# A two-layer fp32 decoder trunk on one core: the first loads put into one queue, and the last columns finished block by block

## The chip, the core and the metric

The kernel runs on one core of a Trainium2 chip. The core has a matrix engine (TensorE, PE in the profile, with its weight loads as PEld), a vector engine (VectorE, DVE), a scalar engine (ScalarE, ACT), GpSimd (POOL) and SyncE (SP), which here only issues DMAs. All five run their own instruction streams and wait for one another through semaphores. The metric is device time in microseconds for one execution, the median of several. TensorE has two clock levels, 1.2 and 2.4 GHz; the profile gives the granted clock as a share of the upper one.

## What is computed

256 tokens (T) of width 2048 (D) pass two layers and a final normalisation, all in float32:

```python
for i in range(DEPTH):                       # 2 layers
    x = x + mixer(rmsnorm(x, mix_g))         # layer 0: stick-breaking attention || gated short convolution
                                             # layer 1: chunked spatial gate || forgetting attention
    x = x + conv_ffn(rmsnorm(x, ffn_g), w_up, conv_w, w_down)
return rmsnorm(x, final_norm_g)

def rmsnorm(x, g):
    return x * lax.rsqrt(jnp.mean(x * x, axis=-1, keepdims=True) + EPS) * g
def conv_ffn(h, w_up, conv_w, w_down):       # w_up 2048 x 11264, w_down 5632 x 2048
    gate, up = jnp.split(causal_dwconv(h @ w_up, conv_w), 2, axis=-1)
    return (jax.nn.silu(gate) * up) @ w_down
```

The weights, some 400 MB in all, are each read once.

## The kernel before, in words

**Tiles.** The residual stream `res[b][g]` stays on the core: two blocks of 128 tokens (b), each in four column groups of 512 (g). Weights come as `raw` tiles of 512 rows by 512 columns (1 MB, `load`, L216) over SP's DMA queue; five `raw` buffers turn round. ACT casts each half of a tile to a rounded `hi` (L233), DVE subtracts to get the rest, `lo` (L234). The activations are held in the same way as a pair hi|lo, `xg` (16 tiles of 128 features, `make_xg`, L186) or `act`.

**Products.** `gemm` (L248) makes features by tokens: for each k-tile (128 rows of the weight) and each of four output tiles one matmul of `hi` with 512 columns (the activation's hi and lo side by side, L238) and one of `lo` with 256 (L241). `gemm_tok` (L277) makes tokens by columns: per k-tile and block three matmuls with 512 columns (L291 to L293). A normalisation's factor is applied after the product, so the first projection needs only x transposed and multiplied by the gain; the row sums of squares are needed later.

**Order.** The code calls each step in a program order; a scheduler then sorts each engine's instructions by that order and its own estimates of when inputs are there. Side jobs (`active`, `waiting`) advance by one step after each half weight tile (`tick`).

**The head.** x comes in eight DMAs of 256 KB (L417), the first weight tile in four of 256 KB, the next two in halves, interleaved on SP's queue by the list `START`. ACT's queue brings the first gain `g0row` (L130), six small rows of other gains into `vrow` (L431 to L433), and, hoisted to the start by the scheduler, `fb` (L531) and `sgb` (L542, 512 KB). `bring_x` transposes one column group of x on PE (L196, tiles `px`), makes four `xg` tiles of it (ACT L188, DVE L189) and squares it on ACT (`squares`, L184, tiles `junk`), two k-tiles of the first projection at a time.

**The tail.** `ffn` (L482) runs 11 up-projection steps in chunks; `down(ci)` multiplies a chunk's result by its rows of `w_down` and adds to `res`. The last call covers three steps, [8, 9, 10], so 12 k-tiles for each column group g. After g's two sums (L339, one a block) `final(g)` squares both blocks (L184) and multiplies them by the final gain (L718). When g = 3 is done for both blocks, eight small operations give the two factors per token (L722, L164 to L172), and block 0's four groups are scaled on DVE (L730), block 1's on ACT (L732), each sent by its own DMA of 256 KB (L733, SP for block 0, ACT for block 1).

Of the kernel before, what the change touches and what calls it, by code (L numbers as in the profile page):

```python
# [36 lines left out]
START = [("x", 0), ("w", 0), ("x", 1), ("w", 1), ("x", 2), ("w", 2), ("x", 3), ("w", 3)]  # L37
# [3 lines left out]
def trunk(  # L41
# [55 lines left out]

    ident = cp.tile([P, P], F32, name="ident")
# [30 lines left out]
    g0row = cp.tile([KD, P], F32, name="g0row")  # L129
    nc.scalar.dma_start(g0row, l0_mix_norm_g.rearrange("(r p) -> r p", p=P))  # L130
# [44 lines left out]
    res = [[cp.tile([P, 512], F32, tag=f"res{b}{g}", name=f"res{b}{g}") for g in range(4)] for b in range(2)]  # L175
# [5 lines left out]
    def squares(g):  # L181
        for b in range(2):
            junk = actp.tile([P, 512], F32, tag="act", name=nm("junk"))
            nc.scalar.activation(junk, res[b][g], AF.Square, accum_out=sst[:, b, g:g + 1])  # L184
# [6 lines left out]

    def to_features(g, i):
        for n in range(4):
            px = at("px")
            for b in range(2):
                nc.tensor.transpose(px[:, b * P:(b + 1) * P], res[b][g][:, n * P:(n + 1) * P], ident)  # L196
            make_xg(px[:, :T], g * 4 + n, i)
# [17 lines left out]

    def load(w, r0, col0, halves=False):  # L216
        raw = rawp.tile([P, 4, 512], F32, tag="raw", name=nm("raw"))
        src = w[r0:r0 + 512, col0:col0 + 512].rearrange("(k p) n -> p k n", p=P)
        if halves:
            step = 1 if halves == 2 else 2  # L220
            for k in range(0, 4, step):
                nc.sync.dma_start(raw[:, k:k + step], src[:, k:k + step])
        else:
            nc.sync.dma_start(raw, src)
        return raw
# [51 lines left out]
    def gemm_tok(w, row0, col0, acts, order=None):  # L277
# [17 lines left out]
        return pss  # L295

# [113 lines left out]
    xr = x.rearrange("(b p) d -> p b d", p=P)  # L410

    for what, j in START:
        if what == "w":
            early.append(load(l0_w_in, j * 512, 0, 2 if j == 0 else j < 3))
            continue
        for b in range(2):
            nc.sync.dma_start(res[b][j], xr[:, b, j * 512:(j + 1) * 512])  # L417

    def bring_x(j):
        if j == 0:  # L420
            pv = at("pv")
            nc.tensor.transpose(pv[:, :KD], g0row, ident[:KD, :KD])
            nc.vector.tensor_copy(g0, pv[:, :KD])
# [58 lines left out]
    def ffn(w_up, conv_w, w_down, done, before=lambda: None):  # L482
# [279 lines left out]
```

## Time and profile before

| what | value |
|---|---|
| time of three runs | 2201.64, 2202.65, 2202.7 us (median 2202.65) |
| the profiled execution: its own time | 2203.05 us |
| its span (first to last instruction) | 2201.3 us |
| PE busy | 2182.9 us, 99% of the span, 11568 matmuls |
| DVE busy, ACT busy | 1471.3 us (67%), 1168.6 us (53%) |
| data moved by DMA | 411.24 MB, 187 GB/s on average |

The span is cut into three stretches for what follows: a head of 30 us, a tail that begins when the last matmul hands over at 2188.7 us, and the middle between them. "Busy" counts an engine's instructions from start to end; matmuls overlap in the array, so that a row of one matmul of 512 columns shows 0.40 us although a new one can start every 0.24 us. A row of a timeline that says x4 stands for four instructions in a row, its length for all four. The bracket at the end of a row is the idle time before it and what ended that.

### The profile page before, as it was taken

The numbers are of one execution on the slowest core, as the hardware profiler recorded it, in microseconds if no ns is written. First come the engines' busy times: TensorE is split into PE (matmuls) and PEld (weight loads), VectorE is DVE, ScalarE is ACT, GpSimd is POOL, SyncE is SP. The second block draws the span as 40 slices with busy tenths as digits, with TensorE's granted clock in tenths as the row PEclk, the third lists the DMA queues.
The fourth block names the chain that finished last, engine by engine and source line by source line (L and its number), as shares of the span: only waits on it lengthen the run. The fifth ranks groups of instructions, "written<-read, shape, count | busy, mean of one in ns | idle before, by whom it ended". The sixth has DMA issues, their size and how long they took to land.

```text
span 2201.3 us, 29434 instructions
## 1 busy us (share of the span) xinstructions
PE 2182.9 (99%) x11568; PEld 1869.9 (85%) x11568; DVE 1471.3 (67%) x2233; ACT 1168.6 (53%) x1719; POOL 5.0 (0%) x18
## 2 busy tenths in 40 slices
PE   8999999999999999999999999999999999999997
PEld 7888888888888888888888888888888888888886
DVE  5556665777667576775655568567785766757675
ACT  6566454655455454554555456555554545545453
POOL 0000000000000000000000000000000000000000
PEclk9999999999999999999999999999999999999999
DMA  8555555555555555555555555655555555555552
GB/s 297 173 173 172 188 186 184 190 191 186 192 190 182 198 185 194 186 174 192 190 190 185 171 172 184 201 176 188 191 192 191 191 191 187 195 189 189 195 173 96
DMA packets 209633, 411.24 MB, mean 187 GB/s; under 512 B 8790, under 2 KB 10454, under 8 KB 209494
## 3 DMA queue, kind: packets, MB, share of 16 engines
q1 hardware_dynamic: 204560, 405.82, 54.6%
q10 hardware_dynamic: 4934, 3.54, 0.5%
q8 instruction: 90, 1.47, 0.3%
q14 instruction: 49, 0.40, 0.1%
HBM read 407.24 MB, written 2.10 MB: 186 GB/s over the span
## 4 chain that ended last, share of the span: by engine, by line
PE 98%; DMA 1%; ACT 0%; DVE 0%; issue 0%; SPq 0%; ACTq 0%
PE mm L238 40%; PE mm L241 20%; PE mm L291 12%; PE mm L293 12%; PE mm L292 12%; PE px L196 1%; DMA raw<-in_l_w_in_dram 0%; PE po L352 0%; DMA vrow<-in_l_sc_conv_w_dram 0%; DMA res<-in_x_dram 0%; PE s L608 0%; PE pf L573 0%; PE pm L688 0%; PE po L353 0%; PE zA L369 0%; ACT res L732 0%
## 5 line engine op out<-in xcount | busy, mean ns | idle before, releaser
L234 DVE TENSOR_TENSOR lo<-raw,hi 128x1024 fp32r<-128x1024 f32 (+1 forms) x770 | 940.0, 1221 | 653.9 <-ACT hi L233 651.9
L233 ACT CAST hi<-raw 128x1024 fp32r<-128x1024 f32 (+1 forms) x770 | 807.6, 1050 | 891.5 <-PE mm L238 473.6
L238 PE MATMUL mm<-xg,hi 128*128 128x512 f32 x3840 | 1209.3, 397 | 0.0
L241 PEld LDWEIGHTS mm<-xg,lo 128*128 128x128 f32 x3840 | 717.7, 188 | 166.2
L241 PE MATMUL mm<-xg,lo 128*128 128x256 f32 x3840 | 756.4, 278 | 0.0
L238 PEld LDWEIGHTS mm<-xg,hi 128*128 128x128 f32 x3840 | 589.4, 189 | 5.2 <-ACT hi L233 0.4
L291 PE MATMUL mm<-hi,act 128*128 128x512 f32 x960 | 373.8, 390 | 0.0
L292 PE MATMUL mm<-lo,act 128*128 128x512 f32 x960 | 373.5, 389 | 0.0
L293 PE MATMUL mm<-hi,act 128*128 128x512 f32 x960 | 373.3, 390 | 0.0
L293 PEld LDWEIGHTS mm<-hi,act 128*128 128x128 f32 x960 | 180.3, 188 | 37.3
L292 PEld LDWEIGHTS mm<-lo,act 128*128 128x128 f32 x960 | 180.3, 188 | 36.8
L291 PEld LDWEIGHTS mm<-hi,act 128*128 128x128 f32 x960 | 180.3, 188 | 36.3
L314 ACT COPY y<-mm 128x256 f32<-128x256 f32 x240 | 88.7, 370 | 48.2 <-PE mm L241 48.1
L315 DVE TENSOR_TENSOR y<-mm,y 128x256 f32<-128x256 f32 x240 | 95.4, 417 | 4.5 <-ACT y L314 4.4
L317 DVE TENSOR_TENSOR y<-y,rstd 128x256 f32<-128x256 f32 x224 | 89.3, 420 | 2.0
L327 ACT ACTIVATE cv<-y,cw 128x256 f32<-128x256 f32 x176 | 80.1, 505 | 12.0 <-DVE y L317 10.6
L330 DVE SCALAR_TENSOR_TENSOR cv<-y,cw,cv 128x254 f32<-128x254 f32 x176 | 80.3, 477 | 0.0
L328 DVE SCALAR_TENSOR_TENSOR cv<-y,cw,cv 128x255 f32<-128x255 f32 x176 | 76.7, 477 | 0.0
L291 PE MATMUL mm<-hi,xg 128*128 128x512 f32 x192 | 75.3, 392 | 0.0
L292 PE MATMUL mm<-lo,xg 128*128 128x512 f32 x192 | 75.2, 391 | 0.0
L293 PE MATMUL mm<-hi,xg 128*128 128x512 f32 x192 | 74.9, 390 | 0.0
L339 DVE TENSOR_TENSOR res<-mm,res 128x512 f32<-128x512 f32 x96 | 61.6, 683 | 11.7 <-PE mm L293 11.7
(204 smaller groups left out, 723.0 us busy)
## 6 DMA issues: line engine op xcount, KB each, us to landing
raw<-in_l_ffn_up_dram SPq DMA_DIRECT2D x176, 1024.0 KB, 4.9
raw<-in_l_ffn_down_dram SPq DMA_DIRECT2D x88, 1024.0 KB, 5.1
raw<-in_l_w_in_dram SPq DMA_DIRECT2D x85, 1024.0 KB, 5.1
raw<-in_l_w_out_dram SPq DMA_DIRECT2D x32, 1024.0 KB, 5.1
res<-in_x_dram SPq DMA_DIRECT2D x8, 256.0 KB, 4.2
raw<-in_l_w_in_dram SPq DMA_DIRECT2D x4, 512.0 KB, 7.6
raw<-in_l_w_in_dram SPq DMA_DIRECT2D x4, 256.0 KB, 2.7
gfin<-in_final_norm_g_dram ACTq DMA_DIRECT2D x2, 512.0 KB, 4.7
```

The lines of the kernel that those rows point to most:

```text
L233: nc.scalar.copy(hi[:, c], rawv[:, c])
L234: nc.vector.tensor_tensor(out=lo[:, c], in0=rawv[:, c], in1=hi[:, c].bitcast(F32), op=ALU.subtract)
L238: nc.tensor.matmul(ps, lhsT=hi, rhs=a.rearrange("p s t -> p (s t)"), start=start, stop=False)
L241: nc.tensor.matmul(ps[:, :T], lhsT=lo, rhs=a[:, 0, :], start=False, stop=stop)
L291: nc.tensor.matmul(pss[b], lhsT=ah, rhs=hi[:, k, :], start=first, stop=False)
L292: nc.tensor.matmul(pss[b], lhsT=ah, rhs=lo[:, k, :], start=False, stop=False)
L293: nc.tensor.matmul(pss[b], lhsT=al, rhs=hi[:, k, :], start=False, stop=last)
L314: nc.scalar.copy(y, ps[:, T:])
L315: nc.vector.tensor_tensor(out=y, in0=ps[:, :T], in1=y, op=ALU.add)
L317: nc.vector.tensor_mul(y, y, rstd)
L327: nc.scalar.activation(a, y, AF.Copy, scale=wc(2))
L330: nc.vector.scalar_tensor_tensor(out=a[:, 2:], in0=y[:, :T - 2], scalar=wc(0), in1=a[:, 2:], op0=ALU.mult, op1=ALU.add)
```

## The change

It has five parts.

1. All of x and the first four weight tiles go through SP's queue in a fixed order, written ahead of everything else: 256 columns of x for both blocks, the first k-tile of the weight, the next 256 columns of x, the second k-tile, and so on. `res` becomes four tiles [128, 2, 512] that hold both blocks, and one DMA brings both. On ACT's queue only `g0row` is left at the start: before each of the loads of `vrow`, `fb` and `sgb` stands a small DVE copy from `rstd` into the destination, so they can't start before the first normalisation's factor exists.
2. The first weight tile is worked off k-tile by k-tile (`first_rows`): per k-tile its `xg`, its cast, its subtraction, four `hi` and four `lo` matmuls. Two k-tiles' transposes share one PSUM tile, here and in later normalisations.
3. The squares leave `bring_x`; a side job `row_sums` makes them, one column group a step, and then runs the normalisation's task.
4. Layer 1's feed-forward part has the chunks [6, 7, 8] and [9, 10] at its end in place of [6, 7] and [8, 9, 10]; the down-projection of the chunk of three is called after the first step of the last chunk, not after the second.
5. The last column group of the last down-projection is done by `gemm_by_block`: its two weight tiles are split into the 16 buffers of `xg`, free by then, first for all eight k-tiles; then come all 24 matmuls of block 0, then the 24 of block 1. `leave(b, ps)` finishes a block behind its matmuls and sends it: the sum, the squares of group 3, six small operations on one column (the sums of groups 0 to 2 are already added up in `part`), four scalings, four DMAs. Group 3's gain is multiplied in the same instruction as its scaling.

```diff
+    g0row = cp.tile([KD, P], F32, name="g0row")
+    nc.scalar.dma_start(g0row, l0_mix_norm_g.rearrange("(r p) -> r p", p=P))
+    nc.sync.dma_start(rest[0][:, :, :256], xr[:, :, :256])
+    nc.sync.dma_start(early[0][:, :1], first_w[:, :1])
+    nc.sync.dma_start(rest[0][:, :, 256:], xr[:, :, 256:512])
+    nc.sync.dma_start(early[0][:, 1:2], first_w[:, 1:2])
+    nc.sync.dma_start(early[0][:, 2:], first_w[:, 2:])
+    for j in range(1, 4):
+        nc.sync.dma_start(rest[j], xr[:, :, j * 512:(j + 1) * 512])
+        early.append(load(l0_w_in, j * 512, 0, ((0, 2), (2, 4)) if j == 1 else ((0, 4),)))
...
+    def first_rows(pss, raw, pre):
+        pieces = transposed(0)
+        for k in range(4):
+            make_xg(pieces[k], k, 0)
...
+            nc.scalar.copy(h, raw[:, k])
+            nc.vector.tensor_tensor(out=l, in0=raw[:, k], in1=h.bitcast(F32), op=ALU.subtract)
+            for n in range(4):
+                mm_hi(pss[n], h[:, n * P:(n + 1) * P], xg[k], k == 0)
+            for n in range(4):
+                mm_lo(pss[n], l[:, n * P:(n + 1) * P], xg[k], False)
+            if k == 1:
+                pre(1)
...
+    def gemm_by_block(w, row0, col0, acts, done):
+        parts = []
+        for j in range(len(acts) // 4):
+            raw = load(w, row0 + j * 512, col0)
+            for k in range(4):
+                kt = j * 4 + k
+                hi, lo = (cp.tile([P, 2, T], F32R, tag=f"xg{i}", name=nm("wl")).rearrange("p s t -> p (s t)")
+                          for i in (kt, kt + 8))
+                nc.scalar.copy(hi, raw[:, k])
+                nc.vector.tensor_tensor(out=lo, in0=raw[:, k], in1=hi.bitcast(F32), op=ALU.subtract)
+                parts.append((hi, lo))
+        for b in range(2):
+            ps = new_ps()
+            for kt, act in enumerate(acts):
...
+            done(b, ps)
...
+    def row_sums():
...
+        for g in range(4):
+            squares(g, shared=junk if g < 2 else None)
+            yield 1
+        yield from norm_task(0)
     def bring_x(j):
...
         to_features(j, 0)
-        squares(j)
-        if j == 3:
-            active.append(norm_task(1))
+        if j == 1:
+            active.append(row_sums())
     def vectors():
+        nc.vector.tensor_copy(vrow, rstd[:NV, :P])
...
-        chunks = [[0, 1], [2, 3], [4, 5], [6, 7], [8, 9, 10]]
+        chunks = [[0, 1], [2, 3], [4, 5], [6, 7, 8], [9, 10]] if tail else [[0, 1], [2, 3], [4, 5], [6, 7], [8, 9, 10]]
...
+        if g == 2:
+            nc.vector.tensor_reduce(out=part, in_=sst[:, :, :3], axis=AX.X, op=ALU.add)
+            nc.vector.tensor_scalar(out=part, in0=part, scalar1=1.0 / D, scalar2=EPS, op0=ALU.mult, op1=ALU.add)
...
+    def leave(b, ps):
+        with tc.high_priority(offset=HP):
+            nc.vector.tensor_add(res[b][3], ps, res[b][3])
+            squares(3, (b,))
...
+            for g in (0, 1, 2, 3):
+                y = res[b][g]
+                if g == 1:
+                    nc.scalar.activation(y, y, AF.Copy, scale=q)
+                elif g == 3:
+                    nc.vector.scalar_tensor_tensor(out=y, in0=y, scalar=q, in1=gfin[1][:, 512:], op0=ALU.mult,
+                                                   op1=ALU.mult)
+                else:
+                    nc.vector.tensor_scalar(out=y, in0=y, scalar1=q, scalar2=None, op0=ALU.mult)
+                (nc.scalar if g == 1 else nc.sync).dma_start(outr[:, b, g * 512:(g + 1) * 512], y)
```

**The head, SP's queue, before.** `res00` is block 0, group 0; `raw_2`, `raw_3` and `raw_4` are the first three weight tiles.

```order
L417 DMA res00_119<-in_x_dram 128x512
L417 DMA res10_123<-in_x_dram 128x512
L222 DMA raw_2_132<-in_l0_w_in_dram 128x512 x4
L417 DMA res01_120<-in_x_dram 128x512
L417 DMA res11_124<-in_x_dram 128x512
L222 DMA raw_3_139<-in_l0_w_in_dram 128x2x512 x2
L417 DMA res02_121<-in_x_dram 128x512
L417 DMA res12_125<-in_x_dram 128x512
L222 DMA raw_4_144<-in_l0_w_in_dram 128x2x512 x2
L417 DMA res03_122<-in_x_dram 128x512
L417 DMA res13_126<-in_x_dram 128x512
```

And now, the same place; `res0` is group 0 of both blocks, `raw_1` the first weight tile:

```order
L111 DMA res0_85<-in_x_dram 128x2x256
L112 DMA raw_1_91<-in_l0_w_in_dram 128x512
L113 DMA res0_85<-in_x_dram 128x2x256
L114 DMA raw_1_91<-in_l0_w_in_dram 128x512
L115 DMA raw_1_91<-in_l0_w_in_dram 128x2x512
L117 DMA res1_86<-in_x_dram 128x2x512
L101 DMA raw_2_98<-in_l0_w_in_dram 128x2x512 x2
L117 DMA res2_87<-in_x_dram 128x2x512
L101 DMA raw_3_102<-in_l0_w_in_dram 128x4x512
L117 DMA res3_88<-in_x_dram 128x2x512
L101 DMA raw_4_105<-in_l0_w_in_dram 128x4x512
```

The first weight piece has moved from third place to second, the second half of group 0 stands behind it, and groups 1 to 3 come as one DMA each.

**The head, ACT, before:** the rows around the second weight tile (`raw_3`); `xg_24` to `xg_30` are the k-tiles of x's second group, `xg_38` and `xg_40` those of the third.

```order
L188 ACTIVATE xg_24_211<-px_23_208,g0_117 128x256
L188 ACTIVATE xg_26_217<-px_25_214,g0_117 128x256
L188 ACTIVATE xg_28_223<-px_27_220,g0_117 128x256
L233 CAST hi_47_306<-raw_3_139 128x1024
L184 ACTIVATE junk_45_302,sst_127<-res02_121 128x512
L184 ACTIVATE junk_46_304,sst_127<-res12_125 128x512
L188 ACTIVATE xg_30_229<-px_29_226,g0_117 128x256
L233 CAST hi_49_326<-raw_4_144 128x1024
L233 CAST hi_61_374<-raw_4_144 128x1024
L188 ACTIVATE xg_38_281<-px_37_278,g0_117 128x256
L188 ACTIVATE xg_40_287<-px_39_284,g0_117 128x256
L184 ACTIVATE junk_59_370,sst_127<-res03_122 128x512
```

And now, first the rows of the second weight tile (`raw_2`): `xg_19`, `20`, `21` and `22` belong to x's second group, in PE's order of use 19, 20, 21, 22; `xg_32` and `xg_33` to the third.

```order
L252 CAST hi_27_237<-raw_2_98 128x1024
L252 CAST hi_36_283<-raw_2_98 128x1024
L210 ACTIVATE xg_19_197<-px_17_187,g0_137 128x256
L210 ACTIVATE xg_21_203<-px_18_192,g0_137 128x256
L210 ACTIVATE xg_32_271<-px_30_261,g0_137 128x256
L210 ACTIVATE xg_20_200<-px_17_187,g0_137 128x256
L210 ACTIVATE xg_22_206<-px_18_192,g0_137 128x256
L210 ACTIVATE xg_33_274<-px_30_261,g0_137 128x256
```

Then the rows that follow, with the third and fourth weight tiles (`raw_3`, `raw_4`) and the last two k-tiles of the third group (`xg_34`, `xg_35`):

```order
L206 ACTIVATE junk_41_327,sst_139<-res2_87 128x512
L252 CAST hi_38_305<-raw_3_102 128x1024
L252 CAST hi_48_351<-raw_3_102 128x1024
L206 ACTIVATE junk_29_257,sst_139<-res0_85 128x512
L206 ACTIVATE junk_50_371,sst_139<-res3_88 128x512
L206 ACTIVATE junk_51_373,sst_139<-res3_88 128x512
L210 ACTIVATE xg_34_277<-px_31_266,g0_137 128x256
L206 ACTIVATE junk_29_257,sst_139<-res0_85 128x512
L252 CAST hi_52_375<-raw_4_105 128x1024
L252 CAST hi_58_407<-raw_4_105 128x1024
L206 ACTIVATE junk_29_257,sst_139<-res1_86 128x512
L210 ACTIVATE xg_35_280<-px_31_266,g0_137 128x256
```

A k-tile of the third group (`xg_32`, from the transposes `px_30`) now stands ahead of the second k-tile of the second group (`xg_20`), and ahead of the third group's last one, `xg_35`, stand four casts and six squares (`junk`; a seventh, `junk_40`, is the row just ahead of this piece).

**The tail, DVE, before:** from the last column group's two sums on; `sm` are the small tiles.

```order
L339 TENSOR_TENSOR res03_122<-mm_3183_18982,res03_122 128x512
L339 TENSOR_TENSOR res13_126<-mm_3184_18983,res13_126 128x512
L718 TENSOR_TENSOR res03_122<-res03_122,gfin_3008_17926 128x512
L718 TENSOR_TENSOR res13_126<-res13_126,gfin_3008_17926 128x512
L722 TENSOR_REDUCE sm_3202_19094<-sst_127 128x2
L164 TENSOR_SCALAR sm_3204_19097<-sm_3202_19094 128x2
L168 RECIPROCAL sm_3206_19101<-sm_3205_19099 128x2
L169 TENSOR_TENSOR sm_3205_19099<-sm_3206_19101 128x2
L170 TENSOR_TENSOR sm_3205_19099<-sm_3205_19099,sm_3204_19097 128x2
L171 TENSOR_SCALAR sm_3205_19099<-sm_3205_19099 128x2
L172 TENSOR_TENSOR sm_3203_19096<-sm_3206_19101,sm_3205_19099 128x2
L730 TENSOR_SCALAR res00_119<-res00_119,sm_3203_19096 128x512
```

And now, block 1's part, which follows block 0's same nine rows:

```order
L796 TENSOR_TENSOR res3_88<-mm_3177_19061,res3_88 128x512
L799 SCALAR_TENSOR_TENSOR sm_3179_19089<-sst_139,part_12704 128x1
L802 RECIPROCAL sm_3181_19091<-sm_3180_19090 128x1
L803 SCALAR_TENSOR_TENSOR sm_3182_19092<-sm_3181_19091,sm_3179_19089 128x1
L804 TENSOR_SCALAR sm_3182_19092<-sm_3182_19092 128x1
L805 TENSOR_TENSOR sm_3182_19092<-sm_3182_19092,sm_3181_19091 128x1
L814 TENSOR_SCALAR res0_85<-res0_85,sm_3182_19092 128x512
L814 TENSOR_SCALAR res2_87<-res2_87,sm_3182_19092 128x512
L811 SCALAR_TENSOR_TENSOR res3_88<-res3_88,sm_3182_19092,gfin_2973_17887 128x512
```

The two blocks' sums no longer stand side by side, the two gain products are gone from between the squares and the factor, and the row of four scalings has become two and one that takes the gain with it.

## Rows read from the trace of the kernel before

**Rows 1.** Windows: stretch, sum; busy us of PE, PEld, DVE, ACT, POOL; PEclk; DMA share, GB/s.
```profile
0.00:30.00 30.00, 23.50 (x122) 19.19 (x123) 18.04 (x40) 21.84 (x45) 2.66 (x15) 1.00 0.90 311
30.00:2188.70 2158.70, 2158.70 (x11445) 1850.46 (x11444) 1447.81 (x2179) 1142.59 (x1665) 2.34 (x3) 1.00 0.55 185
2188.70:2201.30 12.60, 0.67 (x3) 0.20 (x2) 5.48 (x15) 4.17 (x9) 0.00 (x0) 0.66 0.45 166
```

**Rows 2.** Waits of PE: tile, line, releaser; total us, times, longest.
```profile
PE pv L422 <- DMA g0row<-in_l_mix_norm_g_dram: 3.6, 1, 3.6
PE px L196 <- DVE xg L189: 2.1, 3, 1.1
```

**Rows 3.** Timeline of PE, head: start, length, instruction, [idle before <-releaser].
```profile
5.49 0.90 PE L196 MATMUL px<-ident,res 128*128 128x128 f32 x3 [0.80 <-DMA res<-in_x_dram]
...
7.84 3.78 PE L238 MATMUL mm<-xg,hi 128*128 128x512 f32 x8
11.42 1.20 PE L241 MATMUL mm<-xg,lo 128*128 128x256 f32 x8
...
17.26 0.44 PE L196 MATMUL px<-ident,res 128*128 128x128 f32 x2 [1.14 <-DVE xg L189]
...
18.92 0.40 PE L238 MATMUL mm<-xg,hi 128*128 128x512 f32 x1
19.16 0.40 PE L241 MATMUL mm<-xg,lo 128*128 128x256 f32 x2
...
24.22 0.44 PE L196 MATMUL px<-ident,res 128*128 128x128 f32 x2 [0.25 <-DVE xg L189]
```

**Rows 4.** Timeline of ACT, head.
```profile
3.76 0.63 ACT L184 ACTIVATE junk<-res 128x512 f32<-128x512 f32 x1 [1.01 <-DMA res<-in_x_dram]
...
6.10 0.46 ACT L188 ACTIVATE xg<-px,g 128x256 fp32r<-128x256 f32 x1
...
7.17 0.62 ACT L233 CAST hi<-raw 128x512 fp32r<-128x512 f32 x1
...
24.11 0.64 ACT L184 ACTIVATE junk<-res 128x512 f32<-128x512 f32 x1
...
24.72 0.48 ACT L188 ACTIVATE xg<-px,g 128x256 fp32r<-128x256 f32 x1
...
25.52 2.00 ACT L233 CAST hi<-raw 128x1024 fp32r<-128x1024 f32 x2
```

**Rows 5.** Timeline of DVE, head.
```profile
6.58 1.27 DVE L189 SCALAR_TENSOR_TENSOR xg<-px,g,xg 128x256 fp32r<-128x256 f32 x3 [2.56 <-ACT xg L188]
7.82 1.90 DVE L234 TENSOR_TENSOR lo<-raw,hi 128x512 fp32r<-128x512 f32 x3
```

**Rows 6.** Chain that ended last, head: start us, us, what.
```profile
7.45 4.95 DMA vrow<-in_l_sc_conv_w_dram
```

**Rows 7.** DMA of 0 to 45 us, rate in 40 equal slices.
```profile
GB/s 0 55 276 257 382 255 287 193 241 325 219 401 371 251 259 340 402 410 406 390 390 395 377 384 391 382 388 388 390 384 386 386 382 386 362 206 35 0 138 391
```

**Rows 8.** Timeline of all engines, tail.
```profile
2188.72 1.37 DVE L339 TENSOR_TENSOR res<-mm,res 128x512 f32<-128x512 f32 x2 [7.84 <-PE mm L293]
...
2189.45 0.63 ACT L184 ACTIVATE junk<-res 128x512 f32<-128x512 f32 x1 [9.82 <-DVE res L339]
...
2190.21 1.37 DVE L718 TENSOR_TENSOR res<-res,gfin 128x512 f32<-128x512 f32 x2
...
2191.49 0.15 DVE L722 TENSOR_REDUCE sm<-sst 128x2 f32<-128x8 f32 x1
...
2193.11 1.68 DVE L730 TENSOR_SCALAR res<-res,sm 128x512 f32<-128x512 f32 x4
2193.63 2.48 SPq L733 DMA_DIRECT2D out_dram<-res  x4
...
2195.09 2.18 ACTq L733 DMA_DIRECT2D out_dram<-res  x2
```

**Rows 9.** DMA of 2185 to 2201.3 us, rate in 40 equal slices.
```profile
GB/s 0 0 0 0 0 0 0 0 0 0 0 0 0 0 0 0 0 0 0 0 0 0 0 266 382 367 382 387 377 362 392 377 372 392 382 387 322 0 0 0
```

More of the change, by code (lines that the diff above doesn't have):

```diff
@@ L179, in trunk, with squares @@
     xg = [None] * KD
-    def squares(g):
-        for b in range(2):
-            junk = actp.tile([P, 512], F32, tag="act", name=nm("junk"))
+    def squares(g, blocks=(0, 1), shared=None):
+        for b in blocks:
+            junk = shared
+            if shared is None:
+                junk = actp.tile([P, 512], F32, tag="act", name=nm("junk"))
             nc.scalar.activation(junk, res[b][g], AF.Square, accum_out=sst[:, b, g:g + 1])
@@ L213, in norm_task @@
         yield 1
[L216 to L225, printed above, removed]
     def split(rawv, shape=(2, 512), parts=1):
@@ L332, in conv3, with add_res @@
         return a
-    def add_res(w, row0, acts, done=None, order=None):
+    def add_res(w, row0, acts, done=None, order=None, tail=None):
         for g in range(4):
+            if tail and g == 3:
+                gemm_by_block(w, row0, g * 512, acts, tail)
+                return
             pss = gemm_tok(w, row0, g * 512, acts, order)
@@ L407, in stick @@
             yield 1
[L410 to L417, printed above, removed]
+    pv0 = at("pv")
+    nc.tensor.transpose(pv0[:, :KD], g0row, ident[:KD, :KD])
+    nc.vector.tensor_copy(g0, pv0[:, :KD])
+    def row_sums():
+        junk = actp.tile([P, 512], F32, tag="act", name=nm("junk"))
+        nc.vector.tensor_copy(junk[:, :8], xg[7][:, 0, :8].bitcast(F32))
+        for g in range(4):
+            squares(g, shared=junk if g < 2 else None)
+            yield 1
+        yield from norm_task(0)
     def bring_x(j):
[L420 to L423, printed above, removed]
         to_features(j, 0)
-        squares(j)
-        if j == 3:
-            active.append(norm_task(1))
+        if j == 1:
+            active.append(row_sums())
     def vectors():
+        nc.vector.tensor_copy(vrow, rstd[:NV, :P])
         for i, g in enumerate([l0_ffn_norm_g, l1_mix_norm_g, l1_ffn_norm_g, final_norm_g]):
@@ L480, in conv_weights, with ffn @@
             nc.scalar.copy(cw[:, k, :], pt[:, :2 * NF])
-    def ffn(w_up, conv_w, w_down, done, before=lambda: None):
+    def ffn(w_up, conv_w, w_down, done, before=lambda: None, tail=None):
         cw = cp.tile([P, 3, 2 * NF], F32, tag="cw", name=nm("cw"))
@@ L504, in down @@
             k0 = ch[0] * 4
+            last = ci == len(chunks) - 1
             add_res(w_down, k0 * P, [mid[k0 + i] for i in range(4 * len(ch))],
-                    done if ci == len(chunks) - 1 else None)
+                    done if last else None, tail=tail if last else None)
         for ci, ch in enumerate(chunks):
@@ L711, in bring_final_gain, with gained @@
             gfin.append(t)
+    part = cp.tile([P, 2], F32, name="part")
+    def gained(g, b):
+        nc.vector.tensor_mul(res[b][g], res[b][g], gfin[g // 2][:, g % 2 * 512:(g % 2 + 1) * 512])
     def final(g):
-        if g == 2:
+        if g == 1:
             nc.scalar.activation(small(2), sst[:, 0, :2], AF.Sqrt)
@@ L736 @@
+    ffn(l1_ffn_up, l1_ffn_conv_w, l1_ffn_down, final, bring_final_gain, leave)
 _INS = [
```

75 lines of the change are left out of this document (48 added, 27 removed).

## The prediction

> **What bounds the kernel now.** I read the page's busy shares first, then the busy time by stretch [rows 1]. In the middle PE is busy in 2158.70 of 2158.70 us: its stream has no gap. The first 30 us hold 6.5 us without a matmul, and the last 12.6 us hold 0.67 us of matmuls. So time can be won only in these 6.5 and 11.9 us, or by doing less on PE; the change leaves the number of matmuls and their columns as they are (48 matmuls of the last group change their line, not their size). In the middle there is nothing to win and something to lose.
>
> PE's waits come next [rows 2]. 3.6 us go until the first gain row has landed, before any work; the change does not touch that. Three waits for `xg` make 2.1 us, of which 1.14 lie at 17.26 and 0.25 at 24.22 [rows 3], the other 0.7 ahead of the first weight matmul. The first weight matmul starts at 7.84. In the tail [rows 8] the reader should see one chain with PE idle: two sums, two squares, two gain products, eight small operations, four scalings, and behind them 2 MB of output at about 380 GB/s [rows 9].
>
> **The start, step by step.** 256 KB of x land by 3.76 [rows 4]; I take 3.7 for the new first piece, which is as large (3.4 to 4.4: its packets are half as long, which no row prices; the upper end adds the 0.69 us of one more such piece). At 382 GB/s [rows 7] 256 KB follow each 0.69 us, at 255 GB/s each 1.03. The weight piece is there at 4.4, the second x piece at 5.1. On the weight side: cast 0.62 [rows 4] to 5.05, `xg` on ACT 0.46 to 5.5, while DVE subtracts for 0.63 (1.90 for three), then `xg`'s rest on DVE 0.42 (1.27 for three) [rows 5]: 6.1. On PE's side four transposes wait for the second x piece and take 0.9 to 1.2 (0.90 for three [rows 3]): 6.0 to 6.3. The first weight matmul starts at 6.2 rather than 7.84: **1.6 us won** (0.6 to 2.0).
>
> The next matmuls run at half rate: eight `hi` take 3.58 from 7.84 to 11.42, 0.45 each, where one later takes 0.24 (18.92 to 19.16) [rows 3]. That is the 1.2 GHz level, though the stretch prints a granted clock of 1.00 [rows 1]. This costs 8 x 0.21 = 1.7 us before, and I leave it as it is: it starts 1.6 us earlier and lasts as long.
>
> Of the stalls, 1.14 + 0.25 = 1.4 us fall away and one appears. PE comes to the third x group's first transposes (`px_30`) at about 6.2 + 16 x 0.24 + 16 x 0.12 + 1.7 + 12 transposes of some 0.12 = 15.1; x's third group has 3.4 MB ahead of it and itself behind the first piece, which land by 12.6 at 382 GB/s. After `px_30` PE has four matmuls (0.96 us) before it needs `xg_20`. ACT makes `xg_32` first, then `xg_20`, each 0.46 [rows 4], and DVE adds 0.42 [rows 5]: 1.34 us. The stall is 0.4, with the hand-overs 0.5. So 1.4 - 0.5 = **0.9 us won** (0.3 to 1.4). The head gives 2.5 us, between 0.9 and 3.4.
>
> The small loads cost nothing there any more. Before, a 12 KB piece of `vrow` took 4.95 us, and the chain runs through it to SP's next weight load [rows 6]. The Trainium skill, "DMA: Bandwidth & Descriptors", section "Queues, rings and completion order", says that each DMA engine takes turns between the queues of SP and ACT, packet by packet; the trace agrees, with 4.95 us for 12 KB beside SP's queue. The same page, "Two DMAs through the same engine are not ordered", speaks against this change: the order of issue would not be the order of landing (priced under B).
>
> The later `vrow` loads: their last cast on ACT, ahead of them, gets its buffer 48 PE rows before the transposition of `vrow`, 24 x 0.24 + 24 x 0.12 = 8.6 us. The cast takes 1.0 (2.00 for two [rows 4]), six issues 3.7 at the tail's 0.62 each [rows 8]; 3.9 are left for a landing that took 4.95 in the loaded head. The bound is 0 to 2 us; I take 0, since the DMA share in the middle is 0.55 and not 0.90 [rows 1]. `fb` and `sgb` are wanted hundreds of us later.
>
> **The middle.** The new chunk sizes move the same weight tiles about. The last chunk has eight k-tiles per column group where it had twelve, so PE has less to do while ACT and DVE make the last activations. Two column groups' first halves, 2 x 4 k-tiles x 6 matmuls x 0.24 = 11.5 us, cover the conversion of the last four activations; I take 0, with up to 2 us lost.
>
> **The tail.** Call the end of the last matmul E (2188.7 before). Block 0's 24 matmuls are over 24 x 0.24 = 5.7 us before E, and all that follows takes it about 4.3 us to its last issue: its 1 MB moves while block 1 is multiplied and for some 1 us after. Nothing of it is left on the path. Block 1: sum 0.69 (1.37 for two), square 0.76 (2189.45 to 2190.21) [rows 8], six small operations at 0.2 (eight took 1.62, from 2191.49 to 2193.11): E + 2.7. Scaling 0.42 (1.68 for four), then the first issue, E + 3.2; the fourth scaling, with the gain, is done after 0.42 + 0.42 + 0.69 (the 1.37 for two gain products), its issue at E + 4.3. The data began about 0.8 us after the first issue (2193.63; the rate is up in the slice from 2194.4 [rows 9]): E + 4.0. 1.05 MB at 380 GB/s take 2.8: E + 6.8, later than the fourth piece alone could end (4.3 + 0.8 + 0.7 = 5.8). The data before ended near 2200.1 and the span at 2201.3, so 1.2 more: E + 8.0. Before it was E + 12.6: **4.6 us won**. Lower bound 3.8, if the data run at 300 GB/s with one block's four pieces under way; upper 5.3, if each hand-over is as short as a scaling's.
>
> Of this, the outputs give 2.8 (half of 5.6 us of data), the rest is one sum, one square, both gain products and two small operations less; the 0.69 for the gain now lies beside the transfer of the pieces ahead of it. If block 1's data had to queue behind block 0's, up to 1 us of it would come back.
>
> **Sum.** 2.5 + 4.6 = 7.1 us. The profiled execution took 2203.05 (1.75 more than its span), which gives 2195.95. It lies 0.4 above the median of 2202.65; against that, **2195.6 us**.
>
> **Rivals.**
> A. Forecast: both ends gain, 2193.6 to 2197.5.
>
> B. ACT becomes the bound of the first projection. The squares now stand among the casts: ahead of `xg_35`, the twelfth k-tile, ACT has four casts of 512 columns (2.5), six of 1024 (6.0), twelve `xg` (5.5) and seven squares at 0.61 (24.11 to 24.72) [rows 4]: 18.3 us from 4.4, so 22.7 without a wait. PE wants that k-tile after 44 `hi`, 40 `lo` and 24 transposes: 6.2 + 10.6 + 4.8 + 2.9 + 1.7 + 0.5 = 26.7. The last weight tile ends 6.0 MB behind the first piece: 19.5 at 382 GB/s, 27.3 at 255; then two casts, a square, `xg` and its DVE part, 3.5 us. It decides from a landing at 23.2 on, a mean of 309 GB/s, and rows speak for both sides: the first 12 us ran between 193 and 382, the stretch with full queues at 380 to 410 [rows 7]. At 280 GB/s it lands at 25.2, a stall of 2.0; half the head's gain gone, with the outer end at 4: 2197.6 to 2199.6, about 2198. Pieces that land out of their order would show here too: with the first matmul as late as before, the 1.6 would go, 2197.2. That is the case of which the page's second section speaks.
>
> C. A loss in the middle or at the end: the last chunk leaves PE dry, `vrow` is late, or block 0's output is not out early (the change then doesn't do what it says; with block 1's data behind block 0's whole 1 MB, 2.8 us come back). 2 to 6 of the 7.1 us: 2198 to 2201.6. Against it: no PE gap in 2158.70 us [rows 1] with tiles cast well ahead.
>
> D. Slower: TensorE stays at its lower level through the first projection. Before, the rate rose after 3.6 us of matmuls without a gap [rows 3]; now transposes and waits for `xg` stand between groups of four. Price: 64 `hi` at 0.21 more and 64 `lo` at half of that, 13.4 + 6.7 = 20, so 2195.6 + 20 = 2215.6. It is slower than before once a third of them, 7.1 us' worth, run so. Against it: in the head before, the rate stayed up across the stall of 1.14 us. The Trainium skill, "TensorE: Matmul & The Clock Gate", Part 1, says that the low level is the default, that activity releases it and idleness brings it back: the rule by which D would happen. The trace agrees for the first 3.6 us.
>
> **How the numbers follow.** A 0.68, B 0.15, C 0.13, D 0.04. The prediction is A's 2195.6. The range must leave out no more than 0.2: A and B but for their outer edges and the nearer fifth of C, 0.82 in all, 2193.6 to 2199.2. What a measurement here can tell from no change is about 0.2%, 4.4 us: faster means under 2198.2. All of A's range, half of B and a fifth of C lie there: 0.78. Within 0.2%: the rest of B and C, 0.18. Slower: D, 0.04.
>
> **What would show it.** Right: the first weight matmul near 6.2; PE's waits in the head down to one of about 0.5 us behind `px_30`; no wait in the middle; the span's end 8.0 us after the last matmul, block 0's four DMAs done by about E + 1. Wrong: a wait of PE for the twelfth k-tile's `xg` near 26 us (B); PE waiting for `vrow` near 50 us or for `wl` or `act` in the last 60 us, or a first output that starts only with block 1's (C); `hi` matmuls 0.45 us apart after 12 us (D). The forecast would also fail if the first x piece landed later than 4.4, since everything in the head hangs on it.

## The result, and the profile after

The changed kernel takes **2214.28 us** (median of six runs, 2213.53 to 2214.61) against 2202.55 us: a ratio of 1.0053, 95% interval 1.0043 to 1.0063. It is 11.7 us slower. The forecast was 2195.6 us, faster, with a range up to 2199.2; it is wrong by 18.7 us and in its sign.

The two ends are not where this comes from. PE's waits, all of them, in the kernel after (tile, line, releaser; total us, times, longest), beside [rows 2]:

```profile
PE pv L472 <- DMA g0row<-in_l_mix_norm_g_dram: 3.6, 1, 3.6
PE mm L257 <- DVE xg L211: 0.7, 1, 0.7
PE px L221 <- DMA res<-in_x_dram: 0.6, 3, 0.2
```

The kernel before has a third line too, which [rows 2] leaves out:

```profile
PE px L196 <- DMA res<-in_x_dram: 0.8, 1, 0.8
```

The stalls on `xg` are down from 2.1 us to 0.7, and the small loads make nobody wait. The three stretches of the kernel after, cut as in [rows 1]. The tail is taken from 2203.10, 0.2 us after the last matmul's start, when a next one could have started; the end of its row, which is modelled, lies 0.2 us later:

```profile
0.00:30.00 30.00, 25.09 (x134) 20.84 (x135) 18.79 (x36) 22.01 (x45) 2.65 (x15) 1.00 0.95 339
30.00:2203.10 2173.10, 2173.10 (x11437) 1857.91 (x11435) 1450.49 (x2201) 1142.91 (x1674) 2.71 (x3) 1.00 0.55 184
2203.10:2211.80 8.70, 0.20 (x1) 0.00 (x0) 3.09 (x9) 1.65 (x4) 0.00 (x0) 0.79 0.50 187
```

The head has 25.1 us of matmuls in its 30, where it had 23.5. The tail takes 8.7 us. The middle, with no gap before and none after, is what grew: PE is busy in all of it, at a granted clock of 1.00. The time is in the matmuls themselves. Their groups, kernel before, then kernel after (line, engine, operation, shape, count; busy us in total, mean ns of one; idle ahead of them):

```profile
L238 PE MATMUL mm<-xg,hi 128*128 128x512 f32 x3840 | 1209.3, 397 | 0.0
L241 PE MATMUL mm<-xg,lo 128*128 128x256 f32 x3840 | 756.4, 278 | 0.0
```

```profile
L257 PE MATMUL mm<-xg,hi 128*128 128x512 f32 x3840 | 1208.7, 396 | 0.7 <-DVE xg L211 0.7
L260 PE MATMUL mm<-xg,lo 128*128 128x256 f32 x3840 | 768.3, 281 | 0.0
```

The count and the shapes are the same. The `lo` matmuls take 11.9 us more in the sum, though nothing of their code has changed. A second measure has no modelled ends in it: the stretch from 60 to 2150 us, in both kernels full of the same stream. The figure behind x in the PE entry is the number of matmuls that ran in it, those cut by its ends included. Kernel before, then kernel after:

```profile
60.00:2150.00 2090.00, 2090.00 (x11101) 1792.13 (x11100) 1409.53 (x2132) 1111.87 (x1623) 2.34 (x3) 1.00 0.55 187
```

```profile
60.00:2150.00 2090.00, 2090.00 (x11023) 1788.25 (x11022) 1392.23 (x2100) 1099.57 (x1600) 2.71 (x3) 1.00 0.55 186
```

In the same 2090 us the kernel before runs 11101 matmuls and the kernel after 11023. 78 fewer, at 0.188 us each, are 14.7 us.

What had moved is not an instruction but an address. The pools of tiles lie behind each other in the on-chip memory. The change allocates one small new tile, `part`, 8 bytes a partition in a slot of 32, at the end of the first pool. `xg` lies ahead of it and stays at byte 40064 of each partition. `raw`, `hi`, `lo` and `act` lie behind it: `hi` starts at 125344 where it started at 125312. Before, `hi`, `lo` and `act` each lay a whole number of 256 bytes behind `xg` (for `hi` 85248 = 333 x 256); now it is 32 more. These addresses are in the built programs, not in the profile.

### The profile page after: what moved, and what is told of

It reads as the page before. It is cut to its first block, busy times and chain, and to the rows that moved or that the text cites. A ratio compares the mean times of both kernels' runs of the same rounds, so it can differ in the third digit from the quotient of the medians.

```text
span 2211.8 us, 29455 instructions
## 1 busy us (share of the span) xinstructions
PE 2198.4 (99%) x11568; PEld 1878.8 (85%) x11568; DVE 1472.4 (67%) x2246; ACT 1166.6 (53%) x1722; POOL 5.4 (0%) x18
## 4 chain that ended last, share of the span: by engine, by line
PE 99%; DMA 0%; DVE 0%; SPq 0%; ACT 0%; issue 0%; DVEq 0%
PE mm L257 40%; PE mm L260 20%; PE mm L328 12%; PE mm L327 12%; PE mm L329 12%; PE px L221 1%; DMA raw<-in_l_w_in_dram 0%; PE po L413 0%; PE mm L352 0%; PE mm L350 0%; PE pf L636 0%; PE mm L351 0%; PE s L671 0%; PE pm L751 0%; PE po L414 0%; PE zA L430 0%
## 5 line engine op out<-in xcount | busy, mean ns | idle before, releaser
L253 DVE TENSOR_TENSOR lo<-raw,hi 128x1024 fp32r<-128x1024 f32 x762 | 932.0, 1224 | 663.0 <-ACT hi L252 662.1
L252 ACT CAST hi<-raw 128x1024 fp32r<-128x1024 f32 x762 | 800.0, 1050 | 904.3 <-PE mm L257 477.3
L260 PE MATMUL mm<-xg,lo 128*128 128x256 f32 x3840 | 768.3, 281 | 0.0
L328 PE MATMUL mm<-lo,act 128*128 128x512 f32 x944 | 368.0, 390 | 0.0
L327 PE MATMUL mm<-hi,act 128*128 128x512 f32 x944 | 367.5, 390 | 0.0
L329 PE MATMUL mm<-hi,act 128*128 128x512 f32 x944 | 365.8, 389 | 0.0
L329 PEld LDWEIGHTS mm<-hi,act 128*128 128x128 f32 x944 | 177.3, 188 | 36.8
L327 PEld LDWEIGHTS mm<-hi,act 128*128 128x128 f32 x944 | 177.2, 188 | 36.3
L400 DVE TENSOR_TENSOR res<-mm,res 128x512 f32<-128x512 f32 x94 | 60.3, 683 | 8.8 <-PE mm L329 8.8
```

Of the source, the lines that this page charges most:

```text
L252: nc.scalar.copy(hi[:, c], rawv[:, c])
L253: nc.vector.tensor_tensor(out=lo[:, c], in0=rawv[:, c], in1=hi[:, c].bitcast(F32), op=ALU.subtract)
L260: nc.tensor.matmul(ps[:, :T], lhsT=lo, rhs=a[:, 0, :], start=False, stop=stop)
L327: nc.tensor.matmul(pss[b], lhsT=ah, rhs=hi[:, k, :], start=first, stop=False)
L328: nc.tensor.matmul(pss[b], lhsT=ah, rhs=lo[:, k, :], start=False, stop=False)
L329: nc.tensor.matmul(pss[b], lhsT=al, rhs=hi[:, k, :], start=False, stop=last)
```

## The experiments

"Shift" below is the distance by which `hi`, `lo` and `act` lie further from `xg` than in the kernel before: 32 bytes in the changed kernel. Runs that were made together stand beside runs of the kernel before on the same chip (medians of 2202.2 to 2202.4 us). Two theories stood against each other at first: that the place of the tiles makes the matmuls slower (PLACE), and that the change's new order does (ORDER).

**The change with another slot for `part`.** Same instructions in the same order.

```diff
-    part = cp.tile([P, 2], F32, name="part")
+    part = cp.tile([P, 32], F32, name="part")[:, :2]     # a_part128: shift 128
+    part = cp.tile([P, 16], F32, name="part")[:, :2]     # a_part64: shift 64
```

> The changed kernel with the same instructions in the same order; only the tile `part` takes 128 bytes a partition in place of 8, so that all tiles allocated after it (weights raw, hi, lo, and act) start at a multiple of 64 bytes again, as in the kernel before; in the changed kernel they start 32 bytes beside one. Theory PLACE (the 32-byte shift of hi, lo and act against xg makes the matmuls slower: lo matmuls 0.118 us apart in place of 0.115, lo to hi 0.1195 for 0.116, products with xg held fixed 0.235 for 0.228, some 15 us in the sum): about 2199 us, below the kernel before by 3 to 5, with lo matmuls 0.115 apart. Rival ORDER (the change's own order or its held-back loads slow PE, addresses don't matter): 2214 us, unchanged.

> As the run with 128 bytes, but `part` takes 64 bytes: hi, lo and act start at a multiple of 64 but not of 128, xg at a multiple of 128. PLACE with a period of 64 bytes: 2199 us, the same as with 128. PLACE with a period of 128 bytes: slow or partly slow, between 2199 and 2214. ORDER: 2214.

128 bytes: 2201.92 us, ratio 0.9998 (0.9989 to 1.0008). 64 bytes: **2194.20 us**, 0.9962 (0.9949 to 0.9976). The size of a slot that holds 8 bytes of data moves the time by 20 us, from 2214.3 to 2194.2. ORDER falls. PLACE stands, but not in the form expected: 128 missed its 2199 by 3 us, 64 beat it by 5, so it is not a question of starting at a multiple of 64 or not.

**The kernel before, moved.** Only the small tile `st` is larger.

```diff
-    st = cp.tile([P, 2, 2, 6], F32, name="st")
+    st = cp.tile([P, 32], F32, name="st")[:, :24].rearrange("p (a b c) -> p a b c", a=2, b=2)   # b_shift32
+    st = cp.tile([P, 40], F32, name="st")[:, :24].rearrange("p (a b c) -> p a b c", a=2, b=2)   # b_shift64
```

> The kernel before with the same instructions in the same order; only the small tile `st` takes 128 bytes in place of 96, so that raw, hi, lo and act move by 32 bytes, to where the changed kernel has them. PLACE: 2202.5 + 15 = about 2217 us, lo matmuls 0.118 apart. ORDER: 2202.5, unchanged.

> The kernel before with the same instructions and order; `st` takes 160 bytes in place of 96, so that raw, hi, lo and act move by 64 bytes, as in the run with `part` of 64 bytes. PLACE: the middle is 4 to 5 us shorter than in the kernel before, 2197 to 2198.5, and hi matmuls stand 0.227 us apart in place of 0.234. ORDER (the gain of that run is the change's own): 2202.4, unchanged.

Shift 32: 2217.70 us, 1.0068 (1.0052 to 1.0084). Shift 64: 2197.71 us, 0.9979 (0.9970 to 0.9988). Both as PLACE had it. The old kernel, moved by 32 bytes, shows the changed kernel's slow group, 768.3 us there, to within a tenth of a microsecond:

```profile
L241 PE MATMUL mm<-xg,lo 128*128 128x256 f32 x3840 | 768.2, 281 | 0.0
```

**Both moved together.** `sst`, which lies ahead of `xg`, is 32 bytes larger, and `part` takes 128: `xg` moves by 32 bytes and the weight tiles by 160.

```diff
-    sst = cp.tile([P, 2, 4], F32, name="sst")
+    sst = cp.tile([P, 2, 8], F32, name="sst")[:, :, :4]
```

> The changed kernel with `sst` 32 bytes larger and `part` at 128 bytes: xg and hi, lo, act all start 32 bytes beside a multiple of 64, so they stand to each other as in the kernel before. PLACE, relative (only the two operands' places against each other count): 2199 us. PLACE, absolute (an operand that doesn't start at a multiple of 64 is slow by itself): 2214 us or more. ORDER: 2214.

2202.56 us, 0.9999 (0.9989 to 1.0009): not 2199, but the time of the run with shift 128, which is what this one's shift is too (160 - 32). From 60 to 2150 us both run 11086 matmuls. So here the address by itself doesn't count; the distance between `xg` and the tiles behind it does. The profiled execution of this run, 2204.35 us, is the slowest of its ten, for another reason, which is told with the prediction's rival D below.

**The changed kernel at the old addresses.** `part` goes into bytes that the slot of another small tile leaves free. Then the two halves of the change, each alone at the same addresses.

```diff
-    lr = cp.tile([P, 2], F32, name="lr")
...
-    part = cp.tile([P, 2], F32, name="part")      # in a_same; tail_only is made from the kernel before
+    lrp = cp.tile([P, 8], F32, name="lr"); lr, part = lrp[:, :2], lrp[:, 4:6]      # a_same, tail_only
```

> The changed kernel with its order of instructions; only `part` lies in unused bytes of the slot of the small tile `lr`, so that xg, raw, hi, lo and act lie at exactly the addresses of the kernel before. Theory PLACE: the middle runs as in the kernel before, the start gives about 1.5 us and the end 3.5 (both read from the profile of the changed kernel), so 2197.5 to 2199. Forecast as it was on record, had the places not moved: 2195.6. Rival ORDER (the change's order of instructions costs time in the middle, as the 3.3 us between the middles of the 128-byte run and the kernel before could mean): 2201 to 2202.

> The first half of the change alone (loads in one queue, first tile k-tile by k-tile, squares as a side job, held-back small loads), with the kernel before's chunks and end; all tiles from xg on at the addresses of the kernel before. By the profile of the changed kernel 1.5 us are won: 2200.9. By the forecast 2.5: 2199.9. If the new order loses time later: 2202 or more.

> The second half alone (new chunks, last column group by blocks, each block sent by itself), with the kernel before's start, `part` in the slot of `lr`, all tiles at the addresses of the kernel before. By the profile of the changed kernel 3.5 us are won: 2198.9. By the forecast 4.6: 2197.8. If the new chunks lose time in the middle: 2200 or more.

`a_same` takes **2198.62 us**, 0.9982 (0.9974 to 0.9991). `tail_only` takes 2199.00, 0.9985 (0.9976 to 0.9993), as the profile of the changed kernel said. `head_only` takes 2202.02, 0.9998 (0.9989 to 1.0007): 0.4 us, not 1.5, and not to be told from nothing. The middle is now the same in all of them: from 60 to 2150 us the kernel before, `a_same`, `head_only` and `tail_only` run 11101 matmuls each. The new order costs nothing there. `a_same`:

```profile
60.00:2150.00 2090.00, 2090.00 (x11101) 1792.44 (x11100) 1402.35 (x2118) 1109.08 (x1613) 2.70 (x3) 1.00 0.57 187
```

**The other shifts.** `part` at 96, 160, 192 and 224 bytes, one execution each; then 192 timed.

> The changed kernel with `part` at 96 bytes: hi, lo and act move 96 bytes against the kernel before (the changed kernel as it is moves them by 32, the other runs by 0, 64 and 128). If only odd and even multiples of 32 count: slow, 2212 to 2215, as with 32. If each place has its own price: anything between 2194 and 2215; read from the distances of the matmuls.

> `part` at 160 bytes: hi, lo and act move by 160 bytes. Odd multiples of 32 slow: 2212 to 2215. A period of 128 bytes: the same as with 32, 2214.

> `part` at 192 bytes: hi, lo and act move by 192 bytes. A period of 128 bytes: the same as with 64, 2194. Without such a period, but even multiples fast: 2194 to 2202.

> `part` at 224 bytes: hi, lo and act move by 224 bytes. Odd multiples of 32 slow: 2212 to 2215. A period of 128 bytes: the same as with 96.

> The changed kernel with `part` at 192 bytes, the same program as in the one look. If that look holds: 2190.6, 0.9947 of the kernel before. If it was a lucky execution: above 2193.

2218.26, 2218.47, 2190.64 and 2196.81 us. Timed, the shift of 192 gives **2190.20 us**, 0.9944 (0.9927 to 0.9960), the best of all kernels here. Odd multiples of 32 are mostly slow, but 224 is fast, so that rule falls too; each place has its own price, and 128 bytes are no period.

**One of the tiles alone.** From `a_same`; gaps between the pools move one tile by 32 bytes and the tiles behind it by 256 in all.

```text
lo32:  32 bytes ahead of pool lop, 224 ahead of actp; raw, hi at 0, lo at 32, act at 256
hi32:  32 bytes ahead of pool hip, 224 ahead of lop; raw at 0, hi at 32, lo and act at 256
raw32: 32 bytes ahead of pool rawp, 224 ahead of hip; raw at 32, hi, lo and act at 256
```

> The changed kernel with xg at the address of the kernel before, raw alone 32 bytes further, hi, lo and act 256 further. PE doesn't read raw. If only PE's operands count and the pattern repeats after 256 bytes: the four distances as in the kernel before (0.234, 0.233, 0.115, 0.116), 2198.6. RAW: about 2213. If 256 bytes are no period: other distances.

> The changed kernel with xg, raw and hi at the addresses of the kernel before, lo alone 32 bytes further (act 256 bytes further). OWN (a matmul's price goes by its own weight tile's place against xg): both distances behind a lo matmul rise as in the changed kernel, lo to lo 0.115 to 0.118 and lo to hi 0.116 to 0.1195, about 2198.6 + 11.5 = 2210. NEXT (it goes by the next weight tile, loaded while a matmul still streams xg): only lo to lo rises, to 0.118, and hi to lo may change: about 2204. RAW (the place of raw counts): 2198.6.

> The changed kernel with xg and raw at the addresses of the kernel before, hi alone 32 bytes further, lo and act 256 further. OWN: hi to hi and hi to lo stay at 0.234 and 0.233 as they were in the changed kernel, lo to lo and lo to hi stay at 0.115 and 0.116: 2198.6. NEXT: lo to hi rises to 0.1195, 6 us more: about 2205. RAW: 2198.6. If 256 bytes are no whole period of the pattern, lo to lo leaves 0.115.

`raw32`: 2198.86 us, 0.9984 (0.9974 to 0.9994), and 11101 matmuls from 60 to 2150 us, as `a_same`. So the DMA's tiles, which PE doesn't read, don't count, and 256 bytes are a whole period. `lo32`: 2229.78 us, 1.0123 (1.0103 to 1.0143). `hi32`: 2220.68 us, 1.0082 (1.0062 to 1.0102). Both are slower than moving all the tiles together, and both theories on which operand sets the price, OWN and NEXT, fall: neither foresaw 2221 for `hi32` or 2230 for `lo32`, nor that a pair of matmuls none of whose tiles had moved would change. In `lo32` the `hi` matmuls, whose tile had not moved, take 1211.6 us where `a_same` has 1207.3 (238.5 ns from `hi` to `hi`, 234.1 there), and the `lo` matmuls 763.9 for 756.1:

```profile
L257 PE MATMUL mm<-xg,hi 128*128 128x512 f32 x3840 | 1211.6, 397 | 2.0 <-DVE xg L211 2.0
L260 PE MATMUL mm<-xg,lo 128*128 128x256 f32 x3840 | 763.9, 280 | 0.0
```

About half of the loss lies in products that the theories left out, the token-major ones with `act`: their matmuls start 0.231 to 0.236 us apart in `lo32` and 0.231 to 0.232 in `hi32`, in `a_same` 0.227 to 0.228. By these distances they are some 16 of the 31 us in `lo32` and some 12 of the 22 in `hi32`. Where `hi`, `lo` and `act` move together, they keep 0.227 to 0.228 at every shift: there the three stay as they are to each other. The products with `xg` pay in `lo32` and `hi32` about what they pay at shift 32 (the last column below). So it is not one operand's place, but how all tiles that PE reads one after another lie to each other.

Mean distance between the starts of two matmuls in a row, in ns, for each pair of a `hi` matmul (512 columns) and a `lo` (256). It is worked out from the starts in the traces, after 60 us, over 1812 to 1854 pairs each; the last column is the sum of the four.

| shift, kernel | us | matmuls, 60 to 2150 us | hi-hi | hi-lo | lo-lo | lo-hi | sum |
|---|---|---|---|---|---|---|---|
| 0, before | 2202.4 | 11101 | 233.9 | 233.4 | 115.1 | 116.1 | 698.5 |
| 0, a_same | 2198.6 | 11101 | 234.1 | 233.3 | 115.1 | 116.1 | 698.6 |
| 32, b_shift32 | 2217.7 | 11035 | 233.9 | 233.1 | 117.9 | 119.5 | 704.4 |
| 32, the change | 2214.3 | 11023 | 234.1 | 232.9 | 118.0 | 119.5 | 704.5 |
| 64, b_shift64 | 2197.7 | 11120 | 227.2 | 235.9 | 118.6 | 113.8 | 695.5 |
| 64, a_part64 | 2194.2 | 11120 | 227.4 | 235.8 | 118.5 | 113.8 | 695.5 |
| 128, a_part128 | 2201.9 | 11086 | 229.0 | 234.5 | 116.7 | 118.5 | 698.7 |
| 192, best192 | 2190.2 | 11135 | 229.1 | 230.6 | 117.0 | 115.7 | 692.4 |
| `hi` alone 32, hi32 | 2220.7 | 10984 | 235.3 | 232.9 | 116.6 | 118.3 | 703.1 |
| `lo` alone 32, lo32 | 2229.8 | 10935 | 238.5 | 231.1 | 117.7 | 117.6 | 704.9 |

Shift 32 adds 5.9 ns to each four matmuls, some 1850 times: 10.9 us. The products that hold `xg` fixed (576 matmuls of 512 columns) start 229 ns apart at shift 0 and 235 at shift 32, which adds 3.5. Together they are 14.4, where the count of matmuls said 14.7 and the timed pair of the kernel before and `b_shift32` says 15.3. At shift 128 the four are as dear as at 0, and the 3.3 us more lie in the products that hold `xg` fixed: 234 ns, 576 times, is 2.9 us.

## Why the prediction was wrong, point by point

**The middle: the step that failed.** The prediction said that the change leaves the number of matmuls and their columns as they are, that in the middle there is nothing to win, and that at most 2 us are to be lost there by waits. It looked for a loss in waits only and took a matmul's time as given by its shape. The same matmuls became slower by 15 us without a single wait, because a tile of 8 bytes moved the weight tiles. No rival held this: B and C are waits, and D is the clock. D's sign came true and its mechanism did not; the distances of `hi` matmuls fell to 0.23 after some 10 us, as they should.

A small piece of D is on record all the same, in the profile of `x_both32`, which has the changed start. PE, and the window (busy us of PE, PEld, DVE, ACT, POOL; PEclk; DMA share, GB/s):

```profile
16.12 0.63 PE L221 MATMUL px<-ident,res 128*128 128x128 f32 x4 [1.06 <-DMA res<-in_x_dram]
17.40 1.97 PE L257 MATMUL mm<-xg,hi 128*128 128x512 f32 x5 [0.66 <-DVE xg L211]
19.17 0.63 PE L260 MATMUL mm<-xg,lo 128*128 128x256 f32 x2
```

```profile
18.20:21.50 3.30, 3.30 (x12) 2.64 (x11) 1.85 (x5) 3.30 (x8) 0.00 (x0) 0.50 1.05 388
```

Behind two waits, of 1.06 and 0.66 us, the granted clock is 0.50, the level of 1.2 GHz, from 18.2 to 21.5 us. An estimate of its cost is half of these 3.3 us, some 1.7, and this execution lies 1.8 above its run's median. In `a_same`, waits of 0.88 and 0.66 us at the same two places left the clock at 1.00. D happened in one of the 14 profiles with the new start, at a twelfth of its price; what decides it stays open.

At equal places the change is worth the following, from the table: 2202.4 to 2198.6 at shift 0, 2217.7 to 2214.3 at 32, 2197.7 to 2194.2 at 64. That is 3.8, 3.4 and 3.5 us, about half of the 7.1 that were forecast. The other half is two terms of the sum that were mis-sized. The 2198.6 at the old places lies inside the range of 2193.6 to 2199.2, but by luck: in the part that stood for the stalls of B, which did not come.

**The start: 2.5 forecast, about 0.5 measured.** The mechanism came as told; the first weight matmul started at 6.47 in the changed kernel, with 6.2 forecast, and its one stall is 0.66 us, with 0.5 forecast. Three sizes were off. First, the 7.84 of [rows 3], from which 1.6 us were to be won, was a late case: with the same old start, `tail_only` begins at 7.23 and `b_shift32` and `b_shift64` at 7.15 and 7.20. The new start varies as well: in the 14 profiles that have it the first weight matmul comes between 6.42 and 7.49, as the second piece of x lands (PE's wait for it ended at 5.37 in the changed kernel, at 6.56 in `raw32`; 5.1 was forecast). The means are 7.35 and 6.76, 0.6 us apart and not 1.6. `tail_only`, PE (start, length, instruction, idle before):

```profile
7.23 3.52 PE L238 MATMUL mm<-xg,hi 128*128 128x512 f32 x8
10.58 1.11 PE L241 MATMUL mm<-xg,lo 128*128 128x256 f32 x8
11.53 0.86 PE L238 MATMUL mm<-xg,hi 128*128 128x512 f32 x3
```

Second, the prediction let the half-rate stretch start earlier and last as long as before, 3.6 us. Its length varies. In `head_only`, PE:

```profile
6.51 2.08 PE L257 MATMUL mm<-xg,hi 128*128 128x512 f32 x4
8.39 1.06 PE L260 MATMUL mm<-xg,lo 128*128 128x256 f32 x4
9.24 1.91 PE L257 MATMUL mm<-xg,hi 128*128 128x512 f32 x4
10.95 1.04 PE L260 MATMUL mm<-xg,lo 128*128 128x256 f32 x4
11.80 1.11 PE L257 MATMUL mm<-xg,hi 128*128 128x512 f32 x4
12.75 0.64 PE L260 MATMUL mm<-xg,lo 128*128 128x256 f32 x4
```

Four `hi` take 1.88 us from 6.51 to 8.39 and again 1.71 from 9.24 to 10.95, four `lo` 0.85 from 10.95 to 11.80; only then are they at full rate (0.95 for four `hi`). That is 5.3 us at half rate. In the changed kernel as it is, it ended earlier:

```profile
6.47 2.07 PE L257 MATMUL mm<-xg,hi 128*128 128x512 f32 x4
8.35 1.05 PE L260 MATMUL mm<-xg,lo 128*128 128x256 f32 x4
9.20 1.42 PE L257 MATMUL mm<-xg,hi 128*128 128x512 f32 x4
10.46 0.64 PE L260 MATMUL mm<-xg,lo 128*128 128x256 f32 x4
10.93 1.11 PE L257 MATMUL mm<-xg,hi 128*128 128x512 f32 x4
...
16.32 0.97 PE L257 MATMUL mm<-xg,hi 128*128 128x512 f32 x3 [0.66 <-DVE xg L211]
```

Here the second four `hi` take 1.26 and the second four `lo` 0.47. So the length of this stretch differs from one execution to the next: by the starts in the traces, 3.1 to 4.4 us in the four profiles with the old start and 1.5 to 5.3 in the 14 with the new one. A term that takes it as fixed carries an error of about 1 us.

Third, x's third group was to land by 12.6 us. In seven of these 14 profiles PE stood waiting for it at 15 to 16 us, a wait that the sum does not have: 0.25 us at 15.03 in the changed kernel, 0.88 at 15.91 in `a_same`. The foreseen stall of 0.66 comes behind it.

In sum: the 301st matmul starts at 60.8 and 60.3 us in the two profiles with the old start at shift 0 (before, `tail_only`), at 59.8 and 60.0 in two with the new one (`head_only`, `a_same`): 0.65 us. The timed pairs say 0.4, both for `head_only` and for `a_same` against `tail_only`, which is not to be told from nothing.

**The end: 4.6 forecast, 3.4 measured.** `tail_only` gives 3.4. The mechanism held: block 0's four DMAs were issued before block 1's sum, though their data moved until 1.6 us behind the last matmul's end E, with 1 forecast. All engines in the kernel after, from block 1's last matmul:

```profile
2202.91 0.40 PE L352 MATMUL mm<-wl,act 128*128 128x512 f32 x1
2203.34 0.69 DVE L796 TENSOR_TENSOR res<-mm,res 128x512 f32<-128x512 f32 x1 [1.30 <-PE mm L352]
2204.07 0.63 ACT L206 ACTIVATE junk<-res 128x512 f32<-128x512 f32 x1 [2.85 <-DVE res L796]
...
2204.82 0.16 DVE L799 SCALAR_TENSOR_TENSOR sm<-sst,part 128x1 f32<-128x1 f32 x1 [0.79 <-ACT junk L206]
...
2206.09 0.88 DVE L814 TENSOR_SCALAR res<-res,sm 128x512 f32<-128x512 f32 x2
2206.60 1.39 SPq L815 DMA_DIRECT2D out_dram<-res  x3
...
2206.88 0.74 DVE L811 SCALAR_TENSOR_TENSOR res<-res,sm,gfin 128x512 f32<-128x512 f32 x1
```

The rate of the DMA in 40 slices of 0.42 us, from 2195 to 2211.8 us, shows the two blocks' outputs apart; block 0's ends at about 2204.7, block 1's goes from 2207.4 to 2210.2:

```profile
GB/s 0 0 0 0 0 0 0 0 0 0 0 0 0 0 0 0 229 395 376 366 390 380 356 5 0 0 0 0 0 127 400 380 371 385 385 395 54 0 0 0
```

0.5 of the 1.2 us missed are a wrong reading. The prediction took 2188.7 as the end of the last matmul, because DVE's sum starts then [rows 8]. But that is block 0's sum, and [rows 1] itself shows three matmuls behind 2188.70; block 1's last matmul started only at 2188.98:

```profile
2188.98 0.39 PE L293 MATMUL mm<-hi,act 128*128 128x512 f32 x1
```

With E taken 0.2 us after that start, as in the kernel after, the tail before was 2201.3 - 2189.2 = 12.1 us, not 12.6. The rest is many small hand-overs that the row lengths don't hold: the sum starts at E + 0.2, the first issue comes at E + 3.5 (3.2 forecast), the data at E + 4.3 (4.0), the end at E + 8.7 (8.0).

**Terms that were right.** `vrow`: PE transposed it at 49.4 us without a wait, so 0 was right. The last chunk: no wait of PE, so 0 was right. B did not happen: no wait for the twelfth `xg`, in the changed kernel or in any other profile with its start.

## What to carry to other kernels

An edit can change the time of instructions that it doesn't touch: before pricing one, list the tiles that it adds, drops or resizes, and what lies behind them in memory, above all the operands of the busiest engine. When a kernel keeps one engine at 99%, compare the mean length and the count of its instructions before looking for waits; where count, shapes and granted clock are equal and the sum is not, as here, compare the addresses. Here a slot of the right size, mostly unused, was worth more than twice the change itself (2198.6 to 2190.2 us against 2202.4 to 2198.6), so a change of a few microseconds should be compared at equal places, and a start or an end priced from several executions, not from one.

## What the runs showed of the hardware

Matmuls of one shape, back to back at a granted clock of 1.00, do not have one price. 512 columns started on average 227 to 239 ns apart and 256 columns 114 to 121 ns, by the places of the stationary tile, the moving tile and their neighbours in the stream to each other. A shift of 256 bytes gave the distances of shift 0 (`raw32`), and moving all of these tiles by 32 bytes more changed none (`x_both32` and `a_part128`). The Trainium skill, "TensorE: Matmul & The Clock Gate", section "Wait — 56ns, not 53.3ns?", gives one distance for 512 columns at the upper clock, 215.7 ns; no mean distance here comes down to it, and the measured distances decide. What makes these distances stays open; that reads meet in the memory is a guess that no run shows. Moving `lo` alone changed the distance from `hi` to `hi`, which no theory here foresaw, and the four distances of a place are not the sum of two single effects. It was not tried to move `xg`'s 16 tiles against each other, or to look for the best place of `hi`, `lo` and `act` one by one. Of the eight shifts in steps of 32 bytes, 192 was the best (2190.2 us) and 96 and 160 the worst (2218.3 and 2218.5, one execution each): 28 us, 1.3%, for one program.
